# A block of attention, convolution and experts on one core: where the transposes of an expert step's silu products stand

## The chip, the cores and the metric

One core of one Trainium2 chip runs the kernel. The metric is the time of one execution in microseconds (us) of device time; less is better. Sizes of tiles are partitions x elements, all in float32.

## The reference

Two layers of a diffusion backbone on 256 latent tokens and 256 context tokens of width 1024. The part that matters here is the end of the second layer, a mixture of eight experts: each token goes to the best two, by a softmax over their two logits.

```
logits = ut @ router_w
top_val, top_idx = top_k(logits, 2); gate = softmax(top_val)
comb[n, e] = gate of token n for expert e, else 0
for e in range(8):
    he = silu(ut @ w_gate[e]) * (ut @ w_up[e])       # 1024 -> 3584
    y = y + comb[:, e:e+1] * (he @ w_down[e])        # 3584 -> 1024
```

## The kernel before, in words

The first half of the program (the two mixers and the dense layer) runs before the experts and is not touched. Each expert gathers its tokens into `xg`, with room for 96 of them: 64 main slots and 32 for overflow. Overflow work is put under a branch (`where`, L1191 and L1192) that is entered only where an expert has more than 64 tokens; in this run three of the eight do, one in each of the first three pairs.

The experts go in pairs. An expert has seven steps of 512 hidden columns each, and the two experts of a pair take turns, so there are 56 steps. What one step does:

- The way up (`up`, L1136): 32 products of `xg` with the gate weights and the up weights of this step, into one PSUM bank, `pm` (a tile named `mm` in the trace). `up_extra` (L1147) does the same for the overflow slots, under the branch.
- `hidden`: ScalarE takes the silu of the gate half out of PSUM (L1152), VectorE multiplies it with the up half (L1153); the result is the tile `h`, two buffers of it. For overflow there is `hx` (L1155, L1156).
- `turned`: TensorE transposes `h` (L1164) and `hx` (L1166) into a PSUM bank `aux` (two of those); ScalarE and VectorE copy it to the tile `ht` (L1168, L1169), three buffers.
- The way down (`down`, L1185, and `down_extra`, L1177 under the branch): 8 products of `ht` with the down weights, four ahead of the branch and four behind it.

In the program's text the loop already works three steps at once: after the way up of a step it traces `turned` for the step before and the way down for the one before that. What comes first on an engine, however, is set by a scheduler that goes by priority and readiness: it may place an instruction earlier than the text does, unless a dependence forbids it. `issue_after(x)` is such a dependence: what is traced under it stands behind instruction `x` on the same engine.

The weights are the bulk of the data: 336 tiles of 1 MiB, six for each step (two gate, two up, two down), issued by the queue of SyncE (SP, L1053) in the order of the program into a ring of 16 tiles (`mraw`). A load waits until the tile that lay in its place has been read. Gate and up tiles count as read at the join behind the branch. At a pair's end `expert_out` scales the sums and adds them to the tokens (L1085, L1088, L267, products L1098, additions L1102), and `gather` (L1038) fetches the next pair's tokens; both are spread over the steps, a few of their pieces after each.

Of the kernel before, what the change touches and what calls it, by code (L numbers as in the profile page):

```python
# [27 lines left out]
KD = D // P  # L28
L = 256
# [11 lines left out]
MAIN, EXTRA = 64, 32  # L41
# [154 lines left out]
class Trunk:  # L196
# [15 lines left out]
    def mm(self, w=T):  # L212
        t = self.psum.tile([P, 512], F32, name=self.name("mm"), tag="mm", bufs=MMB)
        return t[:, :w]
# [890 lines left out]
    def experts(self, first, early, most=None):  # L1105

        nc, mp = self.nc, self.moe
        ap = self.ap  # L1110
        mm = nc.tensor.matmul
        xgs, slots, more, waiting = {0: first}, {}, {}, []
        px, pm = self.sc(L), self.mm()
        pds, pdxs = [self.sc(), self.mm()], [self.sc(L), self.mm(L)]
        for ps in (px, *pdxs):
            nc.vector.memset(ps, 0.0)

        def steps(n):
            while n and waiting:
                if next(waiting[0], True):  # L1120
                    waiting.pop(0)
                else:
                    n -= 1

        def load(w, e, ft):
            return [early.pop(0) if early else self.expert_load(ap[w][e, ft, half]) for half in range(2)]

        def up(e, ft):
            xg = xgs[e // 2][:, :, e % 2]
            raws = []  # L1130
            for i, w in enumerate(("eg", "eu")):
                raws.append(load(w, e, ft))
                for k in range(KD):
                    for j in range(2):
                        r = raws[i][k // 4][:, k % 4 * 512 + j * L:k % 4 * 512 + (j + 1) * L]
                        mm(pm[MAIN * j:MAIN * (j + 1), i * L:(i + 1) * L], xg[:, k, :MAIN], r,  # L1136
                           start=k == 0, stop=k == KD - 1, tile_position=(0, MAIN * j))
            return raws

        def up_extra(e, raws):  # L1140
            xg = xgs[e // 2][:, :, e % 2]
            for k in range(KD):
                for i in range(2):
                    for j in range(2):
                        r = raws[i][k // 4][:, k % 4 * 512 + j * L:k % 4 * 512 + (j + 1) * L]
                        q = EXTRA * (2 * i + j)
                        mm(px[q:q + EXTRA], xg[:, k, MAIN:], r, start=k == 0, stop=k == KD - 1, tile_position=(0, q))  # L1147

        def hidden():

            h = mp.tile([P, L], F32, name=self.name("h"), tag="h", bufs=2)
            nc.scalar.activation(h, pm[:, :L], AF.Silu)  # L1152
            nc.vector.tensor_mul(h, h, pm[:, L:])  # L1153
            hx = mp.tile([P, L], F32, name=self.name("hx"), tag="hx", bufs=2)
            nc.scalar.activation(hx[64:], px[:64], AF.Silu)  # L1155
            nc.vector.tensor_mul(hx[64:], hx[64:], px[64:])  # L1156
            return h, hx

        def turned(h, hx):

            pt = self.aux()
            for b in range(2):
                f = slice(b * P, (b + 1) * P)
                nc.tensor.transpose(pt[:, f], h[:, f], self.ident)  # L1164
            for b in range(2):
                nc.tensor.transpose(pt[:, L + b * 64:L + (b + 1) * 64], hx[64:, b * P:(b + 1) * P], self.ident[64:, 64:])  # L1166
            ht = mp.tile([P, L + P], F32, name=self.name("ht"), tag="ht", bufs=3)
            nc.scalar.copy(ht[:, :L], pt[:, :L])  # L1168
            nc.vector.tensor_copy(ht[:, L:], pt[:, L:L + P])  # L1169
            return ht  # L1170

        def down_extra(e, ft, ht, raws):
            for k in range(4):
                r, at = raws[k // 2], k % 2 * 1024
                for q in range(4):
                    c = L + k % 2 * 64 + k // 2 * EXTRA
                    mm(pdxs[e % 2][q * EXTRA:(q + 1) * EXTRA], ht[:, c:c + EXTRA], r[:, at + q * L:at + (q + 1) * L],  # L1177
                       start=ft == 0 and k == 0, stop=ft == NFT - 1 and k == 3, tile_position=(0, q * EXTRA))

        def down(e, ft, ht, raws):  # L1180
            for k in range(4):
                r, at = raws[k // 2], k % 2 * 1024
                for n in range(2):
                    c = k % 2 * P + k // 2 * MAIN
                    mm(pds[e % 2][n * MAIN:(n + 1) * MAIN], ht[:, c:c + MAIN], r[:, at + n * 512:at + (n + 1) * 512],  # L1185
                       start=ft == 0 and k == 0, stop=ft == NFT - 1 and k == 3, tile_position=(0, n * MAIN))

        def where(e, *jobs):

            if e not in more:  # L1190
                more[e] = nc.tensor.value_load(self.more[0:1, e:e + 1], min_val=0, max_val=1)  # L1191
            with self.tc.If(more[e] > 0):  # L1192
                for job, *args in jobs:
                    job(*args)

        def finish(e, ft, ht, raws):
            down(e, ft, ht, raws)
            if ft == NFT - 1:
                waiting.append(self.expert_out((pds[e % 2], pdxs[e % 2]), *slots[e]))

        fresh, behind = None, []
        for pair, ft, j in [(pair, ft, j) for pair in range(NE // 2) for ft in range(NFT) for j in range(2)][:most]:
            e = 2 * pair + j
            raws = up(e, ft)
            late, jobs = None, [(up_extra, e, raws)]
            if behind:
                late = behind.pop()
                late += load("ed", *late[:2]),
                if late[0] == e:
                    jobs.insert(0, (down_extra, *late))  # L1210
                else:
                    where(late[0], (down_extra, *late))
            where(e, *jobs)
            h = hidden()
            if fresh:
                behind.append((*fresh[0], turned(*fresh[1])))
            if late:
                finish(*late)
            steps(3)
            if ft == 3:  # L1220
                slots[e] = self.slot_gate(e)
                if j and pair < NE // 2 - 1:
                    waiting.append(self.gather(self.selections(pair + 1)))
            if ft == 5 and j:
                steps(8)
                xgs[pair + 1] = self.gathered
            fresh = (e, ft), h
        late = behind.pop()
        late += load("ed", *late[:2]),
        where(late[0], (down_extra, *late))  # L1230
        finish(*late)
        late = (*fresh[0], turned(*fresh[1]), load("ed", *fresh[0]))
        where(late[0], (down_extra, *late))
        finish(*late)
        steps(16)
# [207 lines left out]
```

## Time and profile before

| | |
|---|---|
| median of three runs | 1789.05 us (1787.66 to 1789.59) |
| the profiled execution's own time | 1784.13 us |
| its span, first to last instruction | 1782.6 us |
| mean granted clock of TensorE, share of full | 0.989 |
| TensorE busy | 1682.3 us, 94% |
| VectorE, ScalarE busy | 608.7 us, 445.1 us |
| read from HBM | 472.55 MB |

The expert stage begins at about 902 us with the first way up and lasts to the end. Busy times are sums over the whole span. Products are pipelined, so a row's time holds some of the next one's; idle time "before" a row is the time in which the engine had nothing in work, with what ended it behind the arrow. A DMA share of 1 means that all 16 DMA engines of the core are moving packets.

### The profile page before, as it was taken

Reading aid. Unit: us, or ns where it says so; the run is one execution under the profiler, and the core shown is the slowest. Engines: PE = TensorE matmul, PEld = TensorE weight load, DVE = VectorE, ACT = ScalarE, POOL = GpSimd, SP = SyncE. Lnnn points to the kernel's source line nnn. Section 1 sums busy time; section 2 is a strip of 40 time slices with the busy share of each in tenths; the row PEclk is TensorE's granted clock in tenths of the full one; section 3 lists DMA queues with packets and bytes.
Section 4 is the critical chain, followed back from the end, with each engine's and each line's share of the span. In section 5 each row is a group of like instructions: output and inputs, shape, how many; then the busy total and the mean of one; then the engine's idle time right before and its main releaser. Section 6 shows DMA issues by size and latency. Waiting matters only on the chain. (4 is left out here: it accounts for less than half of the span.)

```text
span 1782.6 us, 27678 instructions
## 1 busy us (share of the span) xinstructions
PE 1682.3 (94%) x11718; PEld 1087.0 (61%) x11718; DVE 608.7 (34%) x1352; ACT 445.1 (25%) x866; POOL 29.4 (2%) x38
## 2 busy tenths in 40 slices
PE   6999999999999999999889999999999999999997
PEld 3877568877777778885755554454545445444443
DVE  5655876423333324778520100311003110031103
ACT  5443564322222123546410000101001000010101
POOL 0021000000000000011000000000000000000000
PEclk9999999999999999999899999999999999999998
DMA  8521353455555553525369999989999899999996
GB/s 311 184 90 44 142 201 95 154 166 165 165 165 166 165 148 113 191 87 195 142 251 367 385 372 412 386 338 403 375 407 425 358 398 370 415 416 397 425 425 261
DMA packets 86313, 475.92 MB, mean 267 GB/s; under 512 B 9707, under 2 KB 13068, under 8 KB 43148
## 3 DMA queue, kind: packets, MB, share of 16 engines
q1 hardware_dynamic: 85580, 473.12, 69.7%
q8 instruction: 121, 1.98, 0.4%
q10 hardware_dynamic: 576, 0.52, 0.1%
q14 instruction: 36, 0.29, 0.0%
HBM read 472.55 MB, written 1.05 MB: 266 GB/s over the span
## 5 line engine op out<-in xcount | busy, mean ns | idle before, releaser
L1136 PE MATMUL mm<-mraw,xg 128*64 128x256 f32 x3584 | 409.5, 382 | 5.2 <-PEq L1192 2.3
L1136 PEld LDWEIGHTS mm<-mraw,xg 128*64 128x64 f32 x3584 | 254.3, 137 | 135.6 <-issue 9.5
L272 PE MATMUL mm<-xh,wh 128*128 128x512 f32 (+1 forms) x656 | 240.6, 368 | 0.8 <-ACT wh L262 0.4
L274 PE MATMUL mm<-xh,wl 128*128 128x512 f32 (+1 forms) x656 | 237.7, 363 | 0.3 <-DVE wl L263 0.3
L273 PE MATMUL mm<-xl,wh 128*128 128x512 f32 (+1 forms) x656 | 237.8, 363 | 0.1
L262 ACT CAST wh<-raw 128x1024 fp32r<-128x1024 f32 (+1 forms) x124 | 128.0, 1034 | 362.5 <-PE mm L273 345.8
L263 DVE TENSOR_TENSOR wl<-raw,wh 128x1024 fp32r<-128x1024 f32 (+1 forms) x124 | 150.1, 1212 | 139.6 <-ACT wh L262 137.9
L272 PEld LDWEIGHTS mm<-xh,wh 128*128 128x128 f32 x656 | 122.9, 188 | 37.2 <-issue 16.5
L274 PEld LDWEIGHTS mm<-xh,wl 128*128 128x128 f32 x656 | 123.2, 188 | 21.7 <-issue 2.2
L273 PEld LDWEIGHTS mm<-xl,wh 128*128 128x128 f32 x656 | 123.0, 188 | 18.9 <-issue 1.5
L1153 DVE TENSOR_TENSOR h<-h,mm 128x256 f32<-128x256 f32 x56 | 23.6, 422 | 320.4 <-ACT h L1152 320.4
L1185 PE MATMUL sc<-mraw,ht 128*64 128x512 f32 x448 | 109.4, 603 | 3.2 <-PEq L1192 1.4
L1185 PE MATMUL mm<-mraw,ht 128*64 128x512 f32 x448 | 108.6, 603 | 3.2 <-PEq L1192 2.1
L1152 ACT ACTIVATE h<-mm 128x256 f32<-128x256 f32 x56 | 21.5, 383 | 344.4 <-PE mm L1136 344.4
L1156 DVE TENSOR_TENSOR hx<-hx,sc 64x256 f32<-64x256 f32 x56 | 23.8, 425 | 242.4 <-ACT hx L1155 242.1
L1155 ACT ACTIVATE hx<-sc 64x256 f32<-64x256 f32 x56 | 21.0, 375 | 288.2 <-PE sc L1147 177.1
L1147 PE MATMUL sc<-mraw,xg 128*32 128x256 f32 x1344 | 76.4, 379 | 0.0
L1164 PE MATMUL aux<-tab_ident,h 128*128 128x128 f32 x112 | 25.1, 302 | 43.7 <-DVE h L1153 43.5
L1185 PEld LDWEIGHTS sc<-mraw,ht 128*64 128x64 f32 x448 | 30.3, 136 | 53.2 <-issue 40.2
L1185 PEld LDWEIGHTS mm<-mraw,ht 128*64 128x64 f32 x448 | 29.0, 136 | 53.9 <-issue 47.1
L1147 PEld LDWEIGHTS sc<-mraw,xg 128*32 128x32 f32 x1344 | 43.4, 110 | 29.2 <-issue 0.8
L1164 PEld LDWEIGHTS aux<-tab_ident,h 128*128 128x128 f32 x112 | 11.5, 140 | 70.2 <-DVE h L1153 64.5
(330 smaller groups left out, 2039.9 us busy)
## 6 DMA issues: line engine op xcount, KB each, us to landing
mraw<-in_eg_dram SPq DMA_DIRECT2D x112, 1024.0 KB, 12.1
mraw<-in_eu_dram SPq DMA_DIRECT2D x112, 1024.0 KB, 15.3
mraw<-in_ed_dram SPq DMA_DIRECT2D x112, 1024.0 KB, 8.6
modw<-in_mod_dram SPq DMA_DIRECT2D x96, 512.0 KB, 3.8
raw<-in_win_dram SPq DMA_DIRECT2D x40, 512.0 KB, 3.9
raw<-in_fg_dram SPq DMA_DIRECT2D x22, 512.0 KB, 4.5
raw<-in_fu_dram SPq DMA_DIRECT2D x22, 512.0 KB, 4.6
raw<-in_wout_dram SPq DMA_DIRECT2D x16, 512.0 KB, 4.4
```

Source lines behind the costliest of these rows:

```text
L262: nc.scalar.copy(hi, raw)
L263: nc.vector.tensor_sub(lo, raw, hi.bitcast(F32))
L272: mm(ps, w[0], x[0], start=start, stop=False)
L273: mm(ps, w[0], x[1], start=False, stop=False)
L274: mm(ps, w[1], x[0], start=False, stop=stop)
L1136: mm(pm[MAIN * j:MAIN * (j + 1), i * L:(i + 1) * L], xg[:, k, :MAIN], r, start=k == 0, stop=k == KD - 1, tile_position=(0, MAIN * j))
L1147: mm(px[q:q + EXTRA], xg[:, k, MAIN:], r, start=k == 0, stop=k == KD - 1, tile_position=(0, q))
L1152: nc.scalar.activation(h, pm[:, :L], AF.Silu)
L1153: nc.vector.tensor_mul(h, h, pm[:, L:])
L1156: nc.vector.tensor_mul(hx[64:], hx[64:], px[64:])
L1164: nc.tensor.transpose(pt[:, f], h[:, f], self.ident)
L1185: mm(pds[e % 2][n * MAIN:(n + 1) * MAIN], ht[:, c:c + MAIN], r[:, at + n * 512:at + (n + 1) * 512], start=ft == 0 and k == 0, stop=ft == N ...
```

## The change

`up` now also returns its last product, and `turned`, which transposes the `h` and `hx` of the step before, is traced under `issue_after` of it. So those transposes cannot be placed ahead of the end of the following step's way up. Nothing is computed in another way, and no instruction is added or taken out. The tail after the loop, which finishes the last two steps, is as it was.

```
@@ def up(e, ft)
-                        mm(pm[MAIN * j:MAIN * (j + 1), i * L:(i + 1) * L], xg[:, k, :MAIN], r,
-                           start=k == 0, stop=k == KD - 1, tile_position=(0, MAIN * j))
-            return raws
+                        last = mm(pm[MAIN * j:MAIN * (j + 1), i * L:(i + 1) * L], xg[:, k, :MAIN], r,
+                                  start=k == 0, stop=k == KD - 1, tile_position=(0, MAIN * j))
+            return raws, last.ins
...
-            raws = up(e, ft)
+            raws, last = up(e, ft)
...
             if fresh:
-                behind.append((*fresh[0], turned(*fresh[1])))
+                with self.tc.issue_after(last):
+                    behind.append((*fresh[0], turned(*fresh[1])))
```

The scheduler's order on TensorE in a step in the middle of a pair, before. Four rows of L1136 with x8 are one way up; the number behind a tile's name tells tiles apart, and a larger one was made later in the program's text.

```order
L1185 MATMUL mm_7578<-mraw_11492,ht_11416 64x512 x4
L1166 MATMUL aux_11685<-tab_ident,hx_11546 128x64 x2
L1136 MATMUL mm_7576<-mraw_11586,xg_10402 64x256 x8
L1136 MATMUL mm_7576<-mraw_11588,xg_10402 64x256 x8
L1136 MATMUL mm_7576<-mraw_11606,xg_10402 64x256 x8
L1136 MATMUL mm_7576<-mraw_11608,xg_10402 64x256 x8
L1164 MATMUL aux_11800<-tab_ident,h_11679 128x128 x2
L1185 MATMUL sc_7577<-mraw_11626,ht_11554 64x512 x4
L1192 COMPARE_AND_BRANCH
```

The same step now.

```order
L1185 MATMUL mm_7578<-mraw_11492,ht_11416 64x512 x4
L1136 MATMUL mm_7576<-mraw_11586,xg_10402 64x256 x8
L1136 MATMUL mm_7576<-mraw_11588,xg_10402 64x256 x8
L1136 MATMUL mm_7576<-mraw_11606,xg_10402 64x256 x8
L1136 MATMUL mm_7576<-mraw_11608,xg_10402 64x256 x8
L1164 MATMUL aux_11685<-tab_ident,h_11543 128x128 x2
L1166 MATMUL aux_11685<-tab_ident,hx_11546 128x64 x2
L1185 MATMUL sc_7577<-mraw_11626,ht_11554 64x512 x4
L1192 COMPARE_AND_BRANCH
```

Before, the way up of a step was followed at once by the transposes of that same step's `h` (11679), and those of `hx` came behind the whole way down. Now the way up is followed by the transposes of `h` and `hx` of the step before (11543, 11546); the way down behind them has not moved and reads the same `ht` (11554).

On VectorE the same place, before:

```order
L1153 TENSOR_TENSOR h_11543<-h_11543,mm_7576 128x256
L1192 UNCONDITIONAL_BRANCH
L1156 TENSOR_TENSOR hx_11546<-hx_11546,sc_7575 64x256
L1169 COPY ht_11690<-aux_11685 128x128
L1153 TENSOR_TENSOR h_11679<-h_11679,mm_7576 128x256
```

And now:

```order
L1153 TENSOR_TENSOR h_11679<-h_11679,mm_7576 128x256
L1169 COPY ht_11690<-aux_11685 128x128
L1192 UNCONDITIONAL_BRANCH
L1156 TENSOR_TENSOR hx_11682<-hx_11682,sc_7575 64x256
L1153 TENSOR_TENSOR h_11794<-h_11794,mm_7576 128x256
```

The copy of the older step's `ht` (11690) stood ahead of the newer product `h` (11679) and now stands behind it.

TensorE where an output group meets a way up, before (the four rows of L1098 are the group):

```order
L1136 MATMUL mm_7576<-mraw_11312,xg_10402 64x256 x8
L1098 MATMUL aux_11443<-back_10269,ye_11431 128x256
L1098 MATMUL aux_11443<-back_10269,ye_11432 128x256
L1098 MATMUL aux_11443<-back_10269,ye_11431 128x256
L1098 MATMUL aux_11443<-back_10269,ye_11432 128x256
L1136 MATMUL mm_7576<-mraw_11314,xg_10402 64x256 x8
L1136 MATMUL mm_7576<-mraw_11332,xg_10402 64x256 x8
L1136 MATMUL mm_7576<-mraw_11334,xg_10402 64x256 x8
L1164 MATMUL aux_11549<-tab_ident,h_11405 128x128 x2
```

And now:

```order
L1136 MATMUL mm_7576<-mraw_11312,xg_10402 64x256 x8
L1136 MATMUL mm_7576<-mraw_11314,xg_10402 64x256 x8
L1136 MATMUL mm_7576<-mraw_11332,xg_10402 64x256 x8
L1136 MATMUL mm_7576<-mraw_11334,xg_10402 64x256 x8
L1164 MATMUL aux_11411<-tab_ident,h_11269 128x128 x2
L1166 MATMUL aux_11411<-tab_ident,hx_11272 128x64 x2
L1098 MATMUL aux_11443<-back_10269,ye_11431 128x256
L1098 MATMUL aux_11443<-back_10269,ye_11432 128x256
L1098 MATMUL aux_11443<-back_10269,ye_11431 128x256
L1098 MATMUL aux_11443<-back_10269,ye_11432 128x256
```

The group of outputs stood behind the first quarter of the way up and now stands behind the whole of it and the transposes.

## Rows read from the trace of the kernel before

**Rows 1.** The page: busy time by engine; DMA share in 40 slices, in tenths.

```profile
PE 1682.3 (94%) x11718; PEld 1087.0 (61%) x11718; DVE 608.7 (34%) x1352; ACT 445.1 (25%) x866; POOL 29.4 (2%) x38
...
DMA  8521353455555553525369999989999899999996
```

**Rows 2.** Windows, four stretches: length, busy by engine, PE's clock, DMA share, GB/s.

```profile
905.00:1127.70 222.70, 209.99 (x1964) 114.88 (x1960) 22.11 (x65) 19.91 (x51) 0.00 (x0) 1.00 0.95 384
1127.70:1354.40 226.70, 211.27 (x1892) 113.15 (x1892) 33.14 (x89) 22.54 (x55) 0.00 (x0) 1.00 0.95 382
1354.40:1580.90 226.50, 210.89 (x1893) 113.28 (x1893) 32.10 (x85) 22.54 (x55) 0.00 (x0) 1.00 0.96 392
1580.90:1745.00 164.10, 149.75 (x1090) 79.18 (x1092) 27.12 (x73) 17.64 (x44) 0.00 (x0) 1.00 1.00 417
```

**Rows 3.** Windows, finer, in the fourth stretch.

```profile
1610.00:1620.00 10.00, 9.74 (x68) 5.31 (x66) 3.27 (x8) 0.75 (x2) 0.00 (x0) 1.00 0.79 312
1620.00:1750.00 130.00, 118.28 (x862) 61.73 (x858) 13.23 (x42) 12.04 (x32) 0.00 (x0) 1.00 1.01 424
```

**Rows 4.** The page: costliest groups, line L1164 on PE.

```profile
L1164 PE MATMUL aux<-tab_ident,h 128*128 128x128 f32 x112 | 25.1, 302 | 43.7 <-DVE h L1153 43.5
```

**Rows 5.** Timeline, PE with ACT, DVE: start, us, engine, instruction, idle before it.

```profile
1303.42 0.38 ACT L1152 ACTIVATE h<-mm 128x256 f32<-128x256 f32 x1 [6.64 <-PE mm L1136]
1303.83 0.42 DVE L1153 TENSOR_TENSOR h<-h,mm 128x256 f32<-128x256 f32 x1 [6.73 <-ACT h L1152]
1304.31 0.44 PE L1164 MATMUL aux<-tab_ident,h 128*128 128x128 f32 x2 [0.94 <-DVE h L1153]
...
1308.64 0.33 PE L1166 MATMUL aux<-tab_ident,hx 64*128 64x64 f32 x2
1308.90 7.13 PE L1136 MATMUL mm<-mraw,xg 128*64 128x256 f32 x64
1316.97 0.44 PE L1164 MATMUL aux<-tab_ident,h 128*128 128x128 f32 x2 [0.94 <-DVE h L1153]
1317.34 1.94 PE L1185 MATMUL sc<-mraw,ht 128*64 128x512 f32 x8
...
1334.72 0.44 PE L1164 MATMUL aux<-tab_ident,h 128*128 128x128 f32 x2 [0.94 <-DVE h L1153]
```

**Rows 6.** PE's waits 905 to 1580.9, then behind it: us, times, longest.

```profile
PE aux L1164 <- DVE h L1153: 31.3, 35, 0.9
...
PE aux L1164 <- DVE h L1153: 12.2, 13, 0.9
```

**Rows 7.** Timeline of PE near the stage's start, without that wait.

```profile
915.27 7.13 PE L1136 MATMUL mm<-mraw,xg 128*64 128x256 f32 x64 [1.41 <-DVE h L1153]
922.33 0.44 PE L1164 MATMUL aux<-tab_ident,h 128*128 128x128 f32 x2
```

**Rows 8.** Timeline of PE, the second output group of a pair.

```profile
1148.10 0.39 PE L1098 MATMUL aux<-back,ye 96*128 96x256 f32 x1 [0.41 <-ACT ye L267]
1148.82 0.62 PE L1098 MATMUL aux<-back,ye 96*128 96x256 f32 x3 [0.33 <-DVE ye L267]
```

**Rows 9.** The page: DMA issues of down weights (count, KB each, us to landing).

```profile
mraw<-in_ed_dram SPq DMA_DIRECT2D x112, 1024.0 KB, 8.6
```

**Rows 10.** Timeline of PE, the last way up.

```profile
1750.61 1.95 PE L1136 MATMUL mm<-mraw,xg 128*64 128x256 f32 x16 [0.49 <-DMA mraw<-in_eu_dram]
```

**Rows 11.** Window of nearly full DMA share, earlier in the stage.

```profile
1200.00:1250.00 50.00, 46.55 (x397) 25.74 (x395) 6.76 (x26) 4.61 (x12) 0.00 (x0) 1.00 0.99 404
```

**Rows 12.** Waits of the SP queue, which issues the loads, 905 to 1750.

```profile
SPq L1053 <- PE sc L1147: 273.3, 38, 16.9
SPq L1053 <- DMA mraw<-in_eg_dram: 30.5, 16, 2.5
```

**Rows 13.** Window at the stage's start; PE's timeline, the first way up.

```profile
895.00:905.00 10.00, 7.50 (x54) 6.33 (x56) 6.12 (x26) 2.71 (x5) 0.00 (x0) 0.83 0.01 2
...
901.78 8.49 PE L1136 MATMUL mm<-mraw,xg 128*64 128x256 f32 x64 [2.02 <-PEq L1192]
```

## The prediction

> **What bounds the kernel now.** I first read the page: TensorE (PE) is busy for 94% of the span, and in its last half the DMA engines are busy too, at 8 or 9 tenths of nearly every slice [rows 1]. Two engines that near their limit decide together, so I then cut the expert stage, which is all that the change touches, into four stretches at the first product of each `expert_out` [rows 2]. In all four PE is busy for 91 to 94% and its clock is at 1.00, the higher of its two levels (2.4 GHz). The DMA share is 0.95, 0.95, 0.96 and 1.00: in the first three stretches the weights keep up with something to spare, in the last there is hardly anything to spare. What "nothing to spare" means is in finer windows: from 1620 to 1750 the share is 1.01 and 424 GB/s pass, the longest stretch at that share in the trace; the last time that the engines rest is between 1610 and 1620, share 0.79 [rows 3].
>
> Next the costliest groups: the transposes of `h` (L1164) have 43.7 us of idle PE ahead of them, nearly all ended by VectorE's product `h` [rows 4]. The timeline shows how: the way up ends, ScalarE's silu takes 0.38 us, VectorE's product 0.42 us, and only then can PE transpose what it has itself just produced. The gap is 0.94 us in nearly every step [rows 5]. By the waits there are 35 such gaps before 1580.9 and 13 behind it, 48 in all, none over 0.9 [rows 6].
>
> So today PE's own chain bounds the first three pairs of experts, and the fourth (two experts without overflow columns, so little PE work per byte) already lives on what the ring of 16 tiles has stored.
>
> **What the change removes.** The built order shows it doing what it says: between two ways up PE now transposes the `h` of the step before, which VectorE made a whole way up earlier. What a gap costs is more than its 0.94 us, since the transposes otherwise start in the shadow of the last product: where nothing was waited for, the first transpose starts 7.06 us after the start of a way up (915.27 to 922.33) [rows 7]; where it waits, 8.07 us (1308.90 to 1316.97) [rows 5]. So one wait is worth 1.01 us. A plain step now takes 12.66 us (1304.31 to 1316.97), one with overflow columns 17.75 us (to 1334.72); they become 11.65 and 16.74.
>
> Also going: where the scheduler had put a second `expert_out` group into the way up, PE waits 0.41 and 0.33 us for `ye` [rows 8]; the new order puts that group behind the whole way up, so about 0.7 us go once in each pair. The first group of a pair keeps its place and its wait.
>
> **What it adds.** No instruction: the same transposes, copies and DMAs. The pairs of transposes of `h` and `hx` now stand together, 0.37 and 0.26 us as before (1316.97 to 1317.34, 1308.64 to 1308.90) [rows 5]. The copies to `ht` come right behind them and are wanted only one step later, so they are covered by a way up of 7 us. The loads keep their order on SP's queue. Their buffers come free at the branch behind the first four down products, which stands no later against the way up than before, except at the `expert_out` and gather rows, where one or two us of products now stand ahead of it once per pair; the ring covers that as long as it holds tiles. The single bank of the way up (`mm`) must be read by silu and product before the next way up writes it; where too little stands between, that is a wait again (1.41 us ahead of an early way up [rows 7]). In the new order 0.63 us of transposes and two halves of four down products, 1.94 us each [rows 5], stand between, in every step but the first few; that is more than the 0.94 us that the chain takes, so I cost it at nothing; without that cover it would cost those 0.94 us again.
>
> **Where it is given back.** A step needs six tiles of 1024 KB, 6.29 MB [rows 9], which at 424 GB/s is 14.8 us. Two steps become 28.4 us of PE against 29.7 us of DMA: in plain rows the DMA is now the slower one. But over a whole stretch, with gathers and outputs, it is not. The second stretch moved 226.7 us x 382 GB/s = 86.6 MB, which at 424 takes 204.2 us, so 22.5 us are spare; the third 88.8 MB in 209.4 us, 17.1 spare; the first 85.5 MB in 201.7 us, 21.0 spare. Thirteen waits and one `ye` are 13.9 us, less than any of these, and the ring evens out what lies within. The last stretch has 164.1 x (1 - 417/424) = 2.7 us to spare against 13 waits. There the end is set by when the last tile lands, and PE will wait for tiles in place of `h`. It does so already at the very end, 0.49 us ahead of one tile's products [rows 10].
>
> The sum: 35 x 1.01 = 35.4, plus 2 x 0.7 = 1.4 for `ye`, plus about 1 of the 2.7 us of the last stretch (2.1 of them are the one rest at 1610 to 1620, a full ring, which an earlier PE removes only in part): **38 us less**. Against the profiled execution's own 1784.1 us (its span is 1782.6) that is 1746; its own time lies 4.9 us under the median of the three runs, 1789.05, so for runs like these I say **1751 us**.
>
> How fast the DMA engines go when asked all the time is the one price that I cannot read directly. From above: the 424 GB/s of the last 130 us. From below: a window of share 0.99 that passed only 404 GB/s [rows 11]. At 404 the third stretch's 88.8 MB take 219.8 us, so 6.7 us are saved there, the second's 12.3 and the first's 11.1, and the last gives nothing: about 30, less what a ring that never refills loses; I put this end at 26. I take 424 because it held for 130 us on end, and the window at 404 holds pauses of the issuing queue, which waits for PE to free buffers far longer than for landings [rows 12].
>
> The trace passes 424 GB/s into one core [rows 3]. The Trainium skill's page "DMA: Bandwidth & Descriptors", section "Where 436 GB/s comes from", says of HBM to SBUF that the HBM side binds, at some 358 GB/s per core. By that figure the 352 MB of expert weights alone would need an estimated 984 us, more than the stage has taken, and the change would save nothing; the trace disagrees, and 424 is used.
>
> **Rivals.** (1) *Everything is kept.* All 48 waits and the `ye` rows go and the DMA follows: 48 x 1.01 + 2 = 50, or 1739 us. It needs the last stretch's 2.7 us of spare to be 13; against it stands the unbroken share of 1.01. (2) *The DMA is slower under full demand*, as priced above: 26 saved, 1763 us. (3) *The wait moves*: the next way up waits for the bank until `h` is read, 0.94 for 0.94, and the time stays at 1789. It needs the next way up right behind the transposes; the order has that only in the first few steps. (4) *PE's clock falls, and it gets slower.* In the fourth pair PE would rest for 14.8 - 11.65 = 3.2 us per step. The trace shows that the clock can fall with rest: its window from 895 reads 0.83, PE has stood still for 2.02 us, and the way up behind takes 8.49 us in place of 7.13 [rows 13]. If the clock stayed low through a step, PE would need up to twice its 11.65 us, 23.3, against 14.8: 8.5 us lost per such step, so from five on the gain of 38 is gone, and with ten of the pair's fourteen the run takes about 1751 + 85 = 1836 us. Against it: the 3.2 us do not come in one piece, they are spread over six tiles, and the waits for tiles at the end left the clock at 1.00 up to 1750 [rows 3]. [...]
>
> **How the numbers follow.** My forecast has 0.70, rival 1 0.08, rival 2 0.14, rivals 3 and 4 0.04 each. The range reaches from just above rival 1 to just past rival 2: 1742 to 1764; it leaves out rivals 1, 3 and 4. A measurement can tell about 0.2%, 3.6 us, from no change: faster 0.92, same 0.04, slower 0.04.
>
> **What would show it.** In the changed profile PE's idle ahead of L1164 should fall from 43.7 us to about 1 (the last step's). The plain pair of steps should read 28.4 us while the ring holds tiles and 29.7 where it doesn't. Windows before the last stretch should carry about 410 GB/s in place of 382 to 392. New waits of PE for `mraw` should add up to 8 to 14 us, mostly in the last fourteen steps, each about 1 us or less, with the clock at 1.00. I am wrong if DMA waits reach 25 us (rival 2), if they stay under 3 us (rival 1), if L1136 waits for L1153 in every step (rival 3), or if the clock is under 1 in a window of the fourth pair ahead of its last products (rival 4).

## The result, and the profile after

The change takes **1747.51 us** (median of four runs, 1746.36 to 1749.11) against 1789.32 for the kernel before in the same comparison (four runs, 1787.66 to 1792.14): a ratio of 0.9776, 95% interval 0.9759 to 0.9792, so 37 to 43 us less (the two medians alone give 0.9766). The profiled execution took 1746.36 us with a span of 1743.9, 38.7 under the span of before.

The page of the changed kernel: PE's busy time, the DMA share in 40 slices, and the costliest group.

```profile
PE 1672.5 (96%) x11718; PEld 1107.2 (63%) x11718; DVE 608.8 (35%) x1352; ACT 444.2 (25%) x866; POOL 29.4 (2%) x38
...
DMA  8531262455555554532549999999999999999995
...
L1136 PE MATMUL mm<-mraw,xg 128*64 128x256 f32 x3584 | 407.8, 381 | 16.4 <-DMA mraw<-in_eg_dram 6.7
```

Against [rows 1] every slice that lies wholly in the expert stage now shows 9 for the DMA engines, up to the tail, and L1164, which had 43.7 us of idle PE ahead of it [rows 4], is no longer among the costliest groups. The way up leads them as it did before, but its idle time has grown from 5.2 to 16.4 us, most of it ended by a tile of weights.

The groups of L1164, by line:

```profile
L1164 PE MATMUL aux<-tab_ident,h 128*128 128x128 f32 x112 | 24.5, 300 | 0.5 <-DVE h L1153 0.3 <-PEq L1192 0.2
```

Two steps in the middle of a pair, one plain and one with overflow, on PE's timeline (start, us, instruction, idle before it); they answer to [rows 5]:

```profile
1274.05 7.08 PE L1136 MATMUL mm<-mraw,xg 128*64 128x256 f32 x64
1281.06 0.44 PE L1164 MATMUL aux<-tab_ident,h 128*128 128x128 f32 x2
1281.43 0.33 PE L1166 MATMUL aux<-tab_ident,hx 64*128 64x64 f32 x2
1281.69 1.94 PE L1185 MATMUL mm<-mraw,ht 128*64 128x512 f32 x8
1283.79 1.94 PE L1185 MATMUL mm<-mraw,ht 128*64 128x512 f32 x8 [0.16 <-PEq L1192]
1285.53 7.11 PE L1136 MATMUL mm<-mraw,xg 128*64 128x256 f32 x64
1292.57 0.44 PE L1164 MATMUL aux<-tab_ident,h 128*128 128x128 f32 x2
...
1309.16 0.44 PE L1164 MATMUL aux<-tab_ident,h 128*128 128x128 f32 x2
```

From transposes to transposes the plain step takes 11.51 us (1281.06 to 1292.57), where it took 12.66, and the one with overflow 16.59 (to 1309.16) where it took 17.75. Each lost 1.15 to 1.16 us, not 1.01. Piece by piece, from start to start, plain step before and after: transposes of `h` 0.37 and 0.37; first half of the way down 2.09 and 2.10; second half 1.87 and 1.74; transposes of `hx` 0.26 and 0.26; way up to transposes 8.07 and 7.04. So 1.03 are the wait, and 0.13 came from the second half of the way down, which is now followed by a way up in place of the `hx` transposes. That second half before; the `hx` transposes behind it start at 1308.64 [rows 5]:

```profile
1306.77 1.94 PE L1185 MATMUL mm<-mraw,ht 128*64 128x512 f32 x8 [0.16 <-PEq L1192]
```

Windows at the first product of each `expert_out`, the four stretches of [rows 2] (length, PE, PEld, DVE, ACT, POOL, PE's clock, DMA share, GB/s); the fourth is cut shortly before the last tiles land:

```profile
905.00:1118.10 213.10, 208.23 (x1967) 118.94 (x1963) 22.21 (x66) 19.80 (x51) 0.00 (x0) 1.00 0.98 397
1118.10:1329.50 211.40, 207.71 (x1893) 118.37 (x1893) 33.20 (x89) 22.41 (x55) 0.00 (x0) 1.00 0.99 409
1329.50:1540.70 211.20, 207.30 (x1893) 119.43 (x1893) 32.08 (x85) 22.36 (x55) 0.00 (x0) 1.00 1.01 421
1540.70:1710.00 169.30, 153.47 (x1112) 86.01 (x1114) 26.77 (x72) 17.12 (x43) 0.00 (x0) 1.00 1.01 425
```

The second and third stretch are 15.3 us shorter each (226.7 to 211.4, 226.5 to 211.2). The first, counted from the first way up (901.78 before, 902.21 now), is 10.0 us shorter; it had nine of the waits. From 1540.7 to the end of the span it is 203.2 us, where it was 201.7 from 1580.9: the fourth pair gained nothing, it lost 1.5. PE's clock stood at its higher level in all four.

PE's waits from 905 to 1540.7, and behind it (us, times, longest), beside [rows 6]:

```profile
PE aux L1068 <- ACT back L1065: 2.7, 6, 0.5
PE mm L1136 <- DVE h L1153: 1.7, 2, 1.4
...
PE mm L1136 <- DMA mraw<-in_eg_dram: 6.7, 10, 2.2
PE mm L1136 <- DMA mraw<-in_eu_dram: 5.4, 11, 0.5
PE sc L1185 <- DMA mraw<-in_ed_dram: 1.6, 4, 0.4
PE mm L1185 <- DMA mraw<-in_ed_dram: 1.5, 3, 0.7
```

Of the 13 waits for `h` in the fourth pair, 12.2 us, one at the very end is left; in their place stand 15.2 us of waits for tiles (with 0.4 further ahead, 15.6 in all). The timeline of PE shows how a step looks there:

```profile
1639.30 0.44 PE L1164 MATMUL aux<-tab_ident,h 128*128 128x128 f32 x2
...
1642.27 1.94 PE L1185 MATMUL sc<-mraw,ht 128*64 128x512 f32 x8 [0.40 <-DMA mraw<-in_ed_dram]
1644.80 1.95 PE L1136 MATMUL mm<-mraw,xg 128*64 128x256 f32 x16 [0.60 <-DMA mraw<-in_eg_dram]
1647.22 1.95 PE L1136 MATMUL mm<-mraw,xg 128*64 128x256 f32 x16 [0.47 <-DMA mraw<-in_eg_dram]
1649.67 1.95 PE L1136 MATMUL mm<-mraw,xg 128*64 128x256 f32 x16 [0.51 <-DMA mraw<-in_eu_dram]
1652.15 1.95 PE L1136 MATMUL mm<-mraw,xg 128*64 128x256 f32 x16 [0.53 <-DMA mraw<-in_eu_dram]
1654.03 0.44 PE L1164 MATMUL aux<-tab_ident,h 128*128 128x128 f32 x2
```

Five of its six tiles are waited for, about half a microsecond at a time, and the step takes 14.73 us, the time in which six tiles pass. Windows show from when on:

```profile
1470.00:1480.00 10.00, 9.89 (x79) 5.55 (x77) 1.27 (x3) 0.76 (x2) 0.00 (x0) 1.00 0.97 390
...
1480.00:1710.00 230.00, 212.34 (x1654) 119.30 (x1656) 33.70 (x89) 24.07 (x59) 0.00 (x0) 1.00 1.01 425
```

The last rest of the DMA engines ends at 1480, where before it was at 1620 [rows 3]. From there they run without a pause for 230 us at 425 GB/s; the ring lasts until about 1637, where the first of those waits ends, and then PE lives on what lands.

### The profile page after: what moved, and what is told of

It is laid out like the page before. It is cut to its first block, busy times and chain, and to the rows that moved or that the text cites. A ratio compares the mean times of both kernels' runs of the same rounds, so it can differ in the third digit from the quotient of the medians.

```text
span 1743.9 us, 27710 instructions
## 1 busy us (share of the span) xinstructions
PE 1672.5 (96%) x11718; PEld 1107.2 (63%) x11718; DVE 608.8 (35%) x1352; ACT 444.2 (25%) x866; POOL 29.4 (2%) x38
## 3 DMA queue, kind: packets, MB, share of 16 engines
q8 instruction: 121, 1.98, 0.4%
## 5 line engine op out<-in xcount | busy, mean ns | idle before, releaser
L1136 PE MATMUL mm<-mraw,xg 128*64 128x256 f32 x3584 | 407.8, 381 | 16.4 <-DMA mraw<-in_eg_dram 6.7
L1136 PEld LDWEIGHTS mm<-mraw,xg 128*64 128x64 f32 x3584 | 277.9, 137 | 152.8 <-issue 30.3
L1153 DVE TENSOR_TENSOR h<-h,mm 128x256 f32<-128x256 f32 x56 | 23.6, 421 | 408.2 <-ACT h L1152 408.1
L1185 PE MATMUL sc<-mraw,ht 128*64 128x512 f32 x448 | 109.1, 603 | 3.9 <-PEq L1192 1.9
L1185 PE MATMUL mm<-mraw,ht 128*64 128x512 f32 x448 | 108.8, 603 | 3.4 <-DMA mraw<-in_ed_dram 1.5
L1185 PEld LDWEIGHTS sc<-mraw,ht 128*64 128x64 f32 x448 | 28.9, 136 | 56.3 <-issue 39.4
L1185 PEld LDWEIGHTS mm<-mraw,ht 128*64 128x64 f32 x448 | 29.1, 136 | 52.1 <-issue 42.3
L839 DVE SCALAR_TENSOR_TENSOR x_latents<-mm,modT,x_latents 128x256 f32<-128x256 f32 x40 | 18.6, 481 | 95.7 <-PE mm L274 95.7
L353 PE MATMUL sc<-modw,cvec 128*32 128x256 f32 x576 | 45.0, 396 | 3.0 <-DMA modw<-in_mod_dram 2.9
## 6 DMA issues: line engine op xcount, KB each, us to landing
mraw<-in_ed_dram SPq DMA_DIRECT2D x112, 1024.0 KB, 11.1
```

The lines of the kernel that those rows point to most:

```text
L353: self.nc.tensor.matmul(ps[g:g + 32, :L], self.cvec[:, 2 * q + k], w[:, k * 512 + n * L:k * 512 + (n + 1) * L], start=q == 0, stop=q == 3, ...
L1136: last = mm(pm[MAIN * j:MAIN * (j + 1), i * L:(i + 1) * L], xg[:, k, :MAIN], r, start=k == 0, stop=k == KD - 1, tile_position=(0, MAIN * j))
```

## The experiments

The theory: a wait of PE counts in full as long as the DMA engines still rest; from their last rest on, the end is set by the tiles still to come. The rivals: a wait counts wherever it stands; or something in the new order itself holds back part of the gain. The runs come from four comparisons, in which the kernel before had medians of 1785.97 to 1789.32 us; so they stand beside each other by their ratios to it. Profiled executions differ by up to 5 us ahead of the first way up, which starts between 901.78 and 907.08 though nothing ahead of it was touched; so I also give the **stage**, the span less that start: 880.8 us before (1782.6 - 901.78), 841.7 for the change (1743.9 - 902.21).

### The change by halves

```
-                with self.tc.issue_after(last):
+                with (self.tc.issue_after(last) if pair < NE // 2 - 1 else ExitStack()):
```

> The changed order in the first three pairs of experts alone; the fourth pair keeps the order of before. Theory (the fourth pair lives on the DMA, whatever PE waits for): the time is that of the whole change, 1744 to 1751 us beside 1747.5, although PE's 13 or 14 waits for `h` of that pair are back (about 13 us of idle PE ahead of L1164); PE's waits for `mraw` in the last 150 us fall from about 15 us to under 4. Rival (a wait of PE costs its length wherever it stands): 13 x 1.15 = 15 us of the gain are lost, about 1762 us.

Measured 1749.04 us against 1788.58, a ratio of 0.9776 (0.9758 to 0.9794), the very ratio of the whole change. PE's waits of this kernel:

```profile
PE aux L1164 <- DVE h L1153: 12.5, 14, 0.9
...
PE mm L1136 <- DMA mraw<-in_eu_dram: 1.9, 4, 0.5
```

The waits for `h` of the fourth pair are all back and cost nothing that shows: the interval leaves some 3 us, the rival wanted 15. Waits for tiles fall to 4.2 us in all (under 4 was expected). The stage is 841.3 us.

The other half, with `pair == NE // 2 - 1` in the same line:

> The changed order in the fourth pair alone; the first three keep the order of before. Theory (the fourth pair lives on the DMA): 0 to 3 us under before, so 1786 to 1789 us beside 1789.3; in place of the 13 waits for `h` PE waits for `mraw`, 10 to 13 us. Rival (a wait costs its length wherever it stands): 13 x 1.15 = 15 us saved, about 1774 us.

Measured 1785.88 us against 1788.58, a ratio of 0.9988 (0.9977 to 0.9998): 2.7 us by the medians, 0.4 to 4.1 by the interval. PE's waits:

```profile
PE aux L1164 <- DVE h L1153: 30.7, 35, 0.9
...
PE mm L1136 <- DMA mraw<-in_eu_dram: 5.2, 9, 1.5
PE mm L1136 <- DMA mraw<-in_eg_dram: 4.5, 8, 0.6
```

Together the two settle it: thirteen waits are worth 15 us in one pair and 0 to 3 in the other, by who is late next.

### PE with a third less to load

The order of before and of the change, each with this edit (and a ring of 14 tiles):

```
         def load(w, e, ft):
+            if w == "ed":
+                return fixed
+        fixed = []
+        for half in range(2):
+            t = self.deep[1].tile([P, 2048], F32, name=self.name("fixed"), tag=f"fixed{half}")
+            nc.sync.dma_start(t, ap["ed"][0, 0, half])
+            fixed.append(t)
```

> The order of before, and every step takes the first expert's first down tiles, which are loaded once: the loading of the down weights is left out (four tiles a step in place of six, a ring of 14 beside the two fixed tiles). The DMA engines then have a third less to bring. Theory (PE's chain bounds the kernel before, but for its last stretch): the time hardly falls, 1780 to 1788 us; the 48 waits for `h` stay. Rival (the DMA engines bound a good part of it): 1765 or less.

> The changed order, with the same loading of down weights left out. It shows what the change is worth to PE alone. Theory: 48 waits at 1.15 us (1.03 of the wait and 0.13 of the `hx` transposes that no longer part the way down from the way up) are 55, plus 1.4 of `ye`, less 3.7 of the new waits for `back`: about 53 us under the run with the order of before, so about 1730 us, with no waits for `mraw`. Rival (the missing part of the gain is not the DMA but something that the new order costs on PE): the difference stays at the 41 to 42 us of the full kernels.

Measured 1764.26 and 1755.55 us: a difference of 9, which neither theory had. The pair does not compare what it was made for. By its number the first falls to the rival's side (1765 or less), but it no longer has the order of before: among its waits there is none of the transposes for `h`, and those of `h` and `hx` stand together behind the way up, 7.06 us after its start at 1274.83, as in the changed order:

```profile
1281.89 0.44 PE L1172 MATMUL aux<-tab_ident,h 128*128 128x128 f32 x2
1282.26 0.34 PE L1174 MATMUL aux<-tab_ident,hx 64*128 64x64 f32 x2
```

So its number says nothing of either theory. And in both it laced products of the way down into the way up, as this timeline of the second one shows (its L1172 and L1193 are L1164 and L1185 of the change):

```profile
1276.15 0.44 PE L1172 MATMUL aux<-tab_ident,h 128*128 128x128 f32 x2
...
1280.64 0.59 PE L1144 MATMUL mm<-mraw,xg 128*64 128x256 f32 x2
1281.04 0.59 PE L1193 MATMUL sc<-fixed,ht 128*64 128x512 f32 x1
...
1288.47 0.44 PE L1172 MATMUL aux<-tab_ident,h 128*128 128x128 f32 x2
```

This step takes 12.32 us against 11.51, with the DMA engines at a share of about 0.7 and no wait for a tile. What the changed order is worth to PE with free loads was not measured in this way; nearest to it come the second and third stretch above, in which PE waits for tiles for 0.4 us at most: 15.3 us a pair.

### Less work for PE

```
-            with self.tc.If(more[e] > 0):
+            with self.tc.If(more[e] > 1):
```

> The changed order with the overflow branch never entered: the overflow slots' products are left out, some 107 us of PE's work (21 steps at 5.1). Theory (after the change the DMA engines bound nearly all of the stage): the time falls only by what they still rest, 12 us by their share in the windows from 905 to 1500, up to 24 by the GB/s against 425; so 1723 to 1736 us, and PE waits for `mraw` some 90 us. Rival (PE still bounds the first three pairs): 50 us or more are saved, under 1700. It also shows whether PE's clock falls when PE waits about 3 us for tiles in every step: by the theory it stays at 1.00.

Measured 1719.22 us against 1785.97, a ratio of 0.9625 (0.9597 to 0.9654) beside 0.9776: 27 us for some 107 us of work taken out, a little over the upper end of what the theory gave, and far from the rival. Its window over 590 us, and PE's waits:

```profile
1100.00:1690.00 590.00, 512.37 (x3542) 261.01 (x3537) 87.55 (x235) 61.15 (x149) 0.00 (x0) 1.00 1.01 426
```

```profile
PE mm L1136 <- DMA mraw<-in_eu_dram: 38.0, 71, 1.4
PE mm L1136 <- DMA mraw<-in_eg_dram: 27.4, 58, 1.3
```

With 78 us of waits for tiles (the two rows and 12.3 at L1185; some 90 were expected) the clock stayed at 1.00 to 1690: waits of half a microsecond at a time, together 13% of it, did not lower it here.

### The ring

```
-RAW = (3, 13)
+RAW = (3, 9)
```

> The changed order with a ring of 12 tiles in place of 16. Theory (from the last rest of the DMA engines on, the end is set by the tiles still to come at 2.47 us each, and a full ring at that time is the lead that they have): four tiles less of lead are 9.9 us, so about 1757 us, and PE's waits for `mraw` grow by about that. Rival (the ring holds more than is needed): within 2 us of 1747.5.

Measured 1755.60 us against 1785.97, a ratio of 0.9822 (0.9800 to 0.9844): 8 us over the change by the ratios, and 10.4 in the stage (852.1) of the traced execution, which at 1761.08 us was the longest of its four. The other way, with `(3, 15)`:

> The changed order with a ring of 18 tiles in place of 16. Theory (from their last rest on, the DMA engines set the end, and a full ring is their lead): two tiles more at 2.47 us each are 4.9 us, so about 1742.6 us, and PE's waits for `mraw` fall by about that, from 15.6 to some 11. Rival (the lead is not the ring's size but what the issuing queue allows): within 1.5 us of 1747.5.

Measured **1740.89 us** against 1788.72, a ratio of 0.9740 (0.9723 to 0.9757): about 6.4 us under the change by the ratios, faster than both kernels; the stage is 835.4. PE's waits for tiles of the larger ring and, behind it, of the smaller (at the way up alone):

```profile
PE mm L1136 <- DMA mraw<-in_eu_dram: 4.3, 7, 1.2
PE mm L1136 <- DMA mraw<-in_eg_dram: 4.0, 6, 1.5
```

```profile
PE mm L1136 <- DMA mraw<-in_eg_dram: 8.6, 12, 2.0
PE mm L1136 <- DMA mraw<-in_eu_dram: 8.2, 16, 0.8
```

With those at L1185 that is 10.4 us with 18 tiles, 15.6 with 16 and 20.6 with 12. From 16 to 18 it fell by 5.2, as two tiles at 2.47 us give. The smaller ring lost 10 in the stage, of which the waits show 5, half of what was expected; of the rest 1.9 us are one way up of 9.02 us at a lower clock, told below, and 1.4 lie in the second stretch (212.8 in place of 211.4), at whose start the clock is lower too (0.71 from 1125 to 1130): 54 products of a way up take 8.25 us there where they take 6.56 in the change. What the last two microseconds are was not looked for. So the 2.47 us a tile are borne out from 16 to 18 tiles and only roughly from 16 to 12.

### The parts of a step

Only the `h` transposes held back:

```
-        def turned(h, hx):
+        def turned(h, hx, last=None):
...
+            with (self.tc.issue_after(last) if last else ExitStack()):
+                for b in range(2):
+                    nc.tensor.transpose(pt[:, f], h[:, f], self.ident)
```

> The transposes of `h` alone are held behind the next way up; those of `hx` may stand anywhere, as before. It tells whether the step fell by 1.15 us (12.66 to 11.51) rather than by the 1.01 of one wait because the `hx` transposes no longer stand alone between the way down and the way up. Theory: the scheduler puts them back there and the plain step reads about 11.65 us (16.7 with overflow), while the DMA has rests; the whole loses 0.14 x 28 to 36 steps, 3 to 5 us, against the change: about 1751. Rival (the placing of `hx` is worth nothing, the 0.14 has another source): the step stays at 11.5 and the time at 1747.5 within 1 us.

Measured 1749.37 us, a ratio of 0.9790 (0.9772 to 0.9809). It tells nothing of the 0.13 us: the scheduler left the `hx` transposes behind those of `h`, and the plain step reads 11.50 (1282.44 to 1293.94). So it was made once more with `hx` held in its old place:

```
+            pt = None
+            if fresh:
+                pt, t = turned_extra(*fresh[1])
+            with (self.tc.issue_after(t) if fresh else ExitStack()):
+                raws, last = up(e, ft)
```

> The changed order, but the transposes of `hx` are held ahead of the next way up, where they stood before; those of `h` stay behind it as in the change. It parts the two gains of a step: the wait for `h` (1.03 us by the rows) and the `hx` transposes between way down and way up (0.13 us). Theory: PE's idle ahead of L1164 stays at about 0, and the plain step reads 11.64 us in place of 11.51; up to the last rest of the DMA engines, some 36 to 40 steps, that is 4 to 5 us, so about 1752 us beside 1747.5. Rival (the step is shorter for another reason, or the DMA hides it): the step stays at 11.51, or the time within 1.5 us of 1747.5.

Its plain step on PE's timeline:

```profile
1293.09 0.44 PE L1170 MATMUL aux<-tab_ident,h 128*128 128x128 f32 x2
...
1295.55 1.94 PE L1189 MATMUL mm<-mraw,ht 128*64 128x512 f32 x8 [0.16 <-PEq L1196]
1297.42 0.33 PE L1162 MATMUL aux<-tab_ident,hx 64*128 64x64 f32 x2
1297.69 7.13 PE L1136 MATMUL mm<-mraw,xg 128*64 128x256 f32 x64
1304.74 0.44 PE L1170 MATMUL aux<-tab_ident,h 128*128 128x128 f32 x2
```

11.65 us, no wait for `h`, and 1.87 again from the second half of the way down to what follows it: the two gains of a step are parted as the rows had it. The time is another matter: 1762.11 us against 1788.72, a ratio of 0.9850 (0.9834 to 0.9866), 13 us over the change where 4 to 5 were expected. The stretches are 216.0 and 217.7 us in place of 211.4 and 211.2. Fourteen steps at 0.13 explain 1.9 of it in each; PE's waits for `ye` are 9.8 us in all in place of 5.1, the first of each pair 2.1 in place of 1.3. The bank `aux` is held a way up longer here, and PE waits 1.0 us for it at L1162. In the third stretch the clock is lower as well, behind the first of those waits (2.13 us, ahead of 1341.70): 1340 to 1350 reads 0.83, and 12 products of the way up take 2.62 us where the same 12 take 1.52 a pair earlier. That accounts for about 4 and 5 us of the two stretches' 4.6 and 6.5. The whole stage of the traced execution is 852.9 us, 11.2 over the change; the rest, up to the 13 by the ratios, stays open.

### The new wait at L1068

```
-        pg = self.aux(2)[:, 0:1]
+        pg = ps[:, L:L + 1]
```

> The changed kernel, with the one-column product of the slots' gates put into a free column of the bank that its neighbour product already uses, so that two `aux` banks are not wanted at once. In the changed kernel PE waits 3.7 us in eight places at L1068 for `back`. Theory (the end is set by the DMA engines, which rest only until about 1480): that wait goes, and the time falls by what lies ahead of the last rest, 0 to 2 us. Rival (PE's waits count in full): 3.7 us less than the change, about 1744.

Measured 1749.20 us, a ratio of 0.9778 (0.9759 to 0.9796), so no change; but the wait did not go either, 3.7 us as before. This kernel's timeline at one of the eight places:

```profile
1006.04 0.37 ACT L1065 CAST back<-aux 96x256 fp32r<-96x256 f32 x1
1006.15 0.29 DVE L1169 COPY ht<-aux 128x128 f32<-128x128 f32 x1 [0.25 <-ACT ht L1168]
...
1006.47 0.24 PE L1068 MATMUL aux<-comb,sel 128*96 128x1 f32 x1 [0.46 <-ACT back L1065]
```

ScalarE's copy of `back` and VectorE's copy of `ht`, which read the two `aux` banks, end within 0.03 us of each other (1006.41, 1006.44). By these rows the product waits the same in whichever bank it stands. So what the wait is worth stays untested.

## Why the prediction was right

By its own steps:

- **The forecast, 38 us less.** For the profiled executions it said 1784.1 - 38 = 1746, and 1746.36 was measured. For medians it carried over 4.9 us, by which the execution of before lay under its median, and said 1751; that of the change lies only 1.2 under its own, hence 1747.5. The range, 1742 to 1764, holds it. The agreement is in part luck. The stage lost 39.1 us: 10.0 in the first stretch and twice 15.3, where 36.8 were said for the three, and in the last it lost ground, 1.5 us, where 1 was to be gained. The first three were put too low by 3.8 and the last too high by 2.5.
- **35 x 1.01 = 35.4 and 1.4 for `ye`.** The wait was sized by comparing one stretch of code with and without it, and came out at 1.03. What was missing is the 0.13 us of the `hx` transposes' old place; I had counted them as moving at equal cost, by their own 0.37 and 0.26 us, and not looked at what their neighbours take. A stretch should have lost 13.9 and lost 15.3: 13 x 1.03 + 14 x 0.13 + 0.7 = 15.9, less 0.9 for two new waits at L1068, which I had not priced: 15.0. Unpriced too was a wait of the gather's products (L1038) for VectorE's copy of `ht`, three times in the trace of before, 1.0 us in all, and gone from that of the change.
- **DMA spare.** 22.5 and 17.1 us were to spare in the second and third stretch, more than the gain, and it was kept there in full; the third now runs at 421 GB/s, close to the end of its spare.
- **The last stretch, about 1 of 2.7 us.** It lost 1.5. The two halves show the same limit: nothing on top of the first three pairs, 2.7 alone. The change reaches the fourth pair with the DMA engines already 60 us past their last rest.
- **What would show it.** PE's idle ahead of L1164 was to fall to about 1 us and fell to 0.5. The waits for tiles are 15.6 us, 8 to 14 were said; but for 0.4 us they begin at 1637, in the last six steps. Each was to be about 1 us or less, and all but one are (2.16). Ahead of the last stretch about 410 GB/s were said, and 397, 409 and 421 passed. A pair of steps was to read 28.4 and 29.7; they read 28.1, and 29.4 in the end (1639.30 to 1668.74).

The rivals: **everything is kept** (1739) falls with the half that changes the last pair alone. **The DMA is slower under full demand** (404 GB/s, 1763) falls with 425 to 426 over 230 us here and 590 us where overflow was left out. Its price held a slip: it counts 11.1 us as saved in the first stretch, which had nine waits, 9.1 us, to lose, so its three stretches give 28 and not 30. The Trainium skill's page "DMA: Bandwidth & Descriptors", section "Where 436 GB/s comes from", would have put the bound at some 358; the trace disagrees, as before. **The wait moves to the bank `mm`**: L1136 waits for L1153 twice, 1.7 us, as in the first steps of before. **The clock falls** in the fourth pair: it stood at 1.00 to 1710. The Trainium skill's page "TensorE: Matmul & The Clock Gate", section "HAM oscillation — how this bites in real kernels", tells of a kernel whose clock falls at every group of products, behind longer waits for the DMA that come in one piece; no run here has such waits in the expert stage, where the longest for a tile is 2.16 us, so they neither bear it out nor speak against it. The clock can fall behind shorter waits, though: in the kernel with 12 tiles PE waited 1.98 us for one tile, and the window behind it reads

```profile
1615.00:1620.00 5.00, 4.12 (x23) 3.04 (x25) 0.00 (x0) 0.00 (x0) 0.00 (x0) 0.66 1.00 424
```

and that way up took 9.02 us in place of 7.1. In the same execution a wait of 1.30 us for `ye` (ahead of 1122.66) has 0.71 behind it, and in the kernel with the last pair alone a wait as long (ahead of 1128.27) has 0.53 from 1130 to 1135. In the change, waits of 1.28 to 1.30 us for `ye` and one of 2.16 us for a tile (ahead of 1675.79) left the clock at 1.00. So a single wait of 1.3 to 2.1 us can be followed by a slower stretch, and often is not; what decides it stays open. It cost 1.7 to 1.9 us in the kernel with 12 tiles and about 3 in the other: 12.1 us from the wait's end to the start of the way up's last 16 products, where the kernel before took 9.1. The prediction's reason against the rival, that the rest of a step is spread over six tiles, agrees with the kernel without overflow; it was not tried by drawing those rests together.

## What to carry to other kernels

Price a wait per stretch, against the spare of the engine that is late next there: the same edit was worth 15 us in a pair whose weights had 17 to 22 us to spare and nothing in a pair that had 3. Where an in-order engine transposes what it has just produced, putting the older result there instead costs no work and takes the chain of the other engines off its path. And once transfers set the end, their lead is worth trying: two more tiles in the ring gave about 6 us more, where the new order gave nothing in the last pair.

## What the runs showed of the hardware

- A group's place costs time beside its own. With `hx` transposes (64 x 128) behind it, the second half of the way down (products of 128 x 64) takes 1.87 us to what follows; followed directly by the way up it takes 1.74 to 1.77. In the change the first half, too, takes 1.87 us where products of 128 x 32 follow it (1293.20 to 1295.07). The Trainium skill's page "TensorEngine Tiling (Array Packing)", section "Key Properties", says that a change of tiling mode drains TensorE; these rows fit it, with 0.10 to 0.13 us, but no run changed the mode alone.
- Single products of the way down laced into a way up went with steps 0.8 us longer (12.32 against 11.51), though their shapes are those of the blocks on either side. What makes them longer was not tried.
- One core took 426 GB/s from HBM for 590 us on end (1100 to 1690, overflow left out) with PE busy for 87% of it.
